# Second layer's paired projections: the next pair's weights prepared between the products of a pair, and the additions of h shared between GpSimd and VectorE

## The chip, the cores and the metric

The kernel runs on one core of a Trainium2 chip. The metric is the time of one execution on the device in microseconds (us); the median of three runs of the kernel before is 1481.52 us (1481.36 to 1482.64). The engines are TensorE (PE, with its weight loads as PEld), VectorE (DVE), ScalarE (ACT), GpSimd (POOL) and SyncE (SP), which here only issues DMAs. Each engine takes its instructions strictly in its own order; what one needs of another it waits for with a semaphore.

## The reference, cut to what matters

Two layers over 1024 latent and 256 context tokens of width 1024. Each layer normalises and modulates the tokens (h) and multiplies them by one wide input weight. Its columns feed four head groups (neighbourhood attention, latent attention, a spatial-gating MLP, a short convolution) and their gates:

```
hx = modulate(rms_norm(x, norm_g), sh_x, sc_x)
(a_q, a_k, a_v, a_g, b_cq, b_ckv, b_kr, b_g,
 c_u, c_v, c_g, d_b, d_c, d_h, d_g) = jnp.split(hx @ w_in, IN_SPLIT_POINTS, axis=-1)
...
out_d = short_conv(d_b, d_c, d_h, sc_w)
x_new = x + g_x * merge_branches((out_a, out_b, out_c, out_d), (a_g, b_g, c_g, d_g), w_out)
```

In the second layer only the latent rows are put out, so ten of these blocks of 256 columns (cg, dc, dh, db, dg, cq, ak, aq, bg, ag) are multiplied with the 1024 latent tokens alone. That stretch is what changes.

## The kernel before, in words

Features lie on the 128 partitions and tokens along the free axis. The latent tokens are two chunks of 512 (c = 0, 1), the context is chunk 2; h lies as tiles `H[c, kc]` for 8 feature blocks kc. Float32 products are made of three passes: every operand is split into a rounded part (hi, a cast on ACT) and the rest (lo, a subtraction on POOL or DVE; `split`, L362 and L367), and PE adds hi·hi, hi·lo and lo·hi in PSUM.

In the second layer a block of 256 columns and the two token chunks form a product of 2 by 2 blocks, which `proj2` computes with seven block products instead of eight (the scheme of Strassen and Winograd). A product is 12 matmuls of 128x512. For that the right sides have to be prepared once for all ten pairs, and the left sides (the weights) for each pair:

- Right: `right_parts(i)` (L702 on; the addition is L708) adds hi and lo of four tiles of h to full values, `right_sums(i)` (L711 on; L715) subtracts them into four new operands named "1" to "4", which are split again. i runs from 0 to 3. All these additions are on POOL, the subtractions on DVE.
- Left: the weights of a pair come as four quarters of 256 KB (L735, on SP's queue), DVE makes four sums of them (L739 to L742), and seven operands are split (`w_op`). Three pairs of buffers, named wh, wl and wr, hold them. The operands of products 0 to 3 are written ahead of the pair, those of 4 to 6 behind products 0, 2 and 3.

The seven products add into three PSUM banks (x_, y_, z_), with two copies by ACT and one by DVE between (L757), which the next product on the same bank has to wait for.

Ahead of the pairs stands a stretch that is written out by hand and whose matmuls are chained, so that PE keeps the order of the text: ckv for the three chunks, each with a normalisation (sums over squares on PE, L597; a power on POOL, L218, and three small operations on DVE, L220 to L223; a broadcast by transposes on PE, L176; a multiplication and a split, L601 to L604); `cv_gate` of c = 0 and 1 (L536 on DVE, L539 on POOL); ak for the context; ten tiles of av (`av_tile`, L569 and L571), with the preparation of the right sides among them. The rest is ordered by a scheduler that works from the order of the text and from dependencies. It fills each engine's queue when the program is built; on the chip nothing is reordered. Tiles of one tag share a fixed number of buffers (x 20, g 24, wr, wh, wl and st 2 each). PSUM has five banks of the kind b, so a matmul block waits for the evacuation of the fifth before it.

After the tenth pair (ag) the kernel goes on to the attention stage: the scaled-up weights, then keys and queries that were stored to DRAM and are read back by DMAs that POOL issues (L954, L962, L1006).

Of the kernel before, what the change touches and what calls it, by code (L numbers as in the profile page):

```python
# [11 lines left out]
F32R = mybir.dt.float32r  # L12
AF = mybir.ActivationFunctionType
ALU = mybir.AluOpType
# [35 lines left out]
V_NG, V_BM, V_QN, V_KV, V_LN, V_SC, V_FG = 0, 8, 32, 34, 35, 37, 43  # L50
# [46 lines left out]
def backbone(ctx: ExitStack, tc: tile.TileContext, a, yT, dbg=None):  # L97
# [85 lines left out]
    def f(ap):  # L183
        return ap.bitcast(F32)
# [241 lines left out]
    def layer(l, H):  # L426
# [262 lines left out]
                spill(scr["kr"][:, :, o:o + n].rearrange("h p n -> p h n"), f(st[64:128]))  # L689


        nop = [0]
        w_tags = ["wh", "wl", "wr"]

        def w_op(raw, lo_eng="pool"):
            t = T(w_tags[nop[0] % len(w_tags)], [2, 512], F32R)
            nop[0] += 1
            split(t[:, 0, :], t[:, 1, :], raw, lo_eng=lo_eng)
            return t.rearrange("p h (k n) -> p h k n", k=4)

        R = {}

        def right_parts(i):

            t = {}
            for k, (c, kc) in enumerate(((0, i), (1, i), (1, i + 4), (0, i + 4))):
                t[k] = T("x", [512])
                after(pool.tensor_tensor(t[k], f(H[c, kc][:, 0, :]), f(H[c, kc][:, 1, :]), ALU.add), last_split[0])  # L708
            R["11", i], R["21", i], R["22", i] = H[0, i], H[0, i + 4], H[1, i + 4]
            return t  # L710

# [13 lines left out]
                              skip_group_check=True)  # L725
                    n += 1

        def proj2(base, evac, mid={}, raw="x"):

            r = {}  # L730
            for j in range(2):
                t = T("st", [2, 512]) if raw == "st" else None
                for k in range(2):
                    r[j, k] = T("x", [512]) if t is None else t[:, k]
                    sp.dma_start(r[j, k], a["wtb"][l, BLOCKS.index(f"{base}{j}")][:, k * 512:(k + 1) * 512])  # L735
            qt = T("wr", [2, 512]) if "wr" not in w_tags else None
            q = [T("x", [512]) if qt is None else qt[:, k] for k in range(2)]
            a11, a12 = w_op(r[0, 0]), w_op(r[0, 1])
            dve.tensor_tensor(q[1], r[0, 0], r[1, 0], ALU.subtract)  # L739
            dve.tensor_tensor(r[1, 0], r[1, 0], r[1, 1], ALU.add)  # L740
            dve.tensor_tensor(q[0], r[1, 0], r[0, 0], ALU.subtract)
            dve.tensor_tensor(r[0, 1], r[0, 1], q[0], ALU.subtract)  # L742
            ops = {0: a11, 1: a12, 2: w_op(q[0], "dve"), 3: w_op(r[1, 0])}
            later = {0: (4, q[1], "dve"), 2: (5, r[0, 1], "dve"), 3: (6, r[1, 1], "pool")}
            x_, y_, z_ = PS("b", [512]), None, None

            def step(n, p, name, first=True):
                for fn in mid.get(n, []):
                    fn()
                product(p, ops[n], name, first)  # L750
                if n in later:
                    k, src, eng = later[n]
                    ops[k] = w_op(src, eng)

            def kept_copy(eng, p):
                t = T("tmp", [512])
                (eng.copy if eng is act else eng.tensor_copy)(t, p)  # L757
                return t

            step(0, x_, "11")  # L760
            m1 = kept_copy(act, x_)
            y_ = PS("b", [512])
            step(1, y_, "21")
            dve.tensor_tensor(m1, y_, m1, ALU.add)
            evac(0, m1, 0)
            step(2, x_, "2", False)
            u2 = kept_copy(act, x_)
            z_ = PS("b", [512])
            step(3, z_, "1")
            z5 = kept_copy(dve, z_)  # L770
            step(4, x_, "3", False)
            dve.tensor_tensor(z5, x_, z5, ALU.add)
            evac(1, z5, 1)
            step(5, z_, "22", False)
            dve.tensor_tensor(u2, z_, u2, ALU.add)
            evac(1, u2, 0)
            step(6, x_, "4", False)
            evac(0, x_, 1)

        def block_c(name, c, evac, **k):  # L780

# [5 lines left out]
        def standard():  # L787
# [51 lines left out]
            for j in range(2):  # L839
                proj(f"bg{j}", all_chunks, lambda c, p: act.activation(map_(2 + j, c), p, AF.Silu))  # L840

        def paired():
            wav = w_tok(a["wav"][l], 288, ("o", "o"), ("o", "o"))
            pe.chain(True)
# [18 lines left out]
                fns.pop(0)()  # L863
            av_tile(8, wav)
            late[-1].pop()()
            parts.append(right_parts(1))
            for t in (9, 4):
                av_tile(t, wav)
            cv_gate(1)
# [7 lines left out]
                av_tile(t, wav)  # L877
            pe.chain(False)
            av_windows()
            proj2("cg", lambda c, p, j: gate(c, p, 4 + j))  # L880
            park((4, 5))
            proj2("dc", lambda c, p, j: act.copy(map_(6 + j, c), p))
            kr = kr_rotate()
            z = {}

            def conv_in(c, p, j):
                z[j, c] = T("x", [512])
                dve.tensor_tensor(z[j, c], p, map_(6 + j, c), ALU.mult)

            proj2("dh", conv_in)  # L890
            kr_transpose(*kr)
            for j in range(2):
                w = [v[:, V_SC + 3 * j + i:V_SC + 3 * j + i + 1] for i in range(3)]
                for c in range(2):
                    m = map_(6 + j, c)
                    act.activation(m, z[j, c], AF.Copy, scale=w[1])
                    for d, s_, k in ((m[:, 1:], z[j, c][:, :511], 0), (m[:, :511], z[j, c][:, 1:], 2),
                                     (m[:, 0:1], z[j, 0][:, 511:], 0) if c else (m[:, 511:], z[j, 1][:, 0:1], 2)):
                        dve.scalar_tensor_tensor(d, s_, w[k], d, ALU.mult, ALU.add)

            def mulb(c, p, j):
                m = map_(6 + j, c)
                dve.tensor_tensor(m, p, m, ALU.mult)

            proj2("db", mulb)
            proj2("dg", lambda c, p, j: gate(c, p, 6 + j))
            park((6, 7))
            proj2("cq", cq_evac)
            proj2("ak", k_evac)
            proj2("aq", lambda c, p, j: q_evac(c, p, j, 0.125))  # L910
            cq_stats()
            w_tags.remove("wr")
            proj2("bg", lambda c, p, j: act.activation(map_(2 + j, c), p, AF.Silu))

        agw = []

# [8 lines left out]

        if last:
            ph = Phase("prj", ("o",))
            paired()
        else:
            standard()  # L930
            ag_weights()
# [535 lines left out]
        order = (0, 1) if last else (2, 0, 1)  # L1467
        if last:
            pe.chain(True)
            proj2("ag", lambda c, p, j: act.activation(map_(j, c), p, AF.Silu),  # L1470
                  {1: [mla_load], 6: [lambda: mla_keys(0)]})
# [218 lines left out]
```

## Time and profile before

| | us |
|---|---|
| runs: median (lowest, highest) | 1481.52 (1481.36, 1482.64) |
| profiled execution, its own time | 1482.33 |
| its span, first to last instruction | 1480.5 |
| PE busy in the span | 1398.0 (94%) |
| DVE busy | 867.8 (59%) |
| ACT busy | 607.6 (41%) |
| POOL busy | 500.0 (34%) |
| mean granted clock of TensorE | 0.988 |

The profile is of one execution. Times of rows are microseconds from the start of its span; 1.8 us of the execution lie outside the span. The stretch of this change goes from about 856 us (the first addition of h) to about 1143 us (the end of the tenth pair). A row of the timeline gives the start, the duration of the whole group, the engine, the line, the operation with its tiles, how many instructions are merged, and in brackets how long the engine was idle before it and who ended that. A granted clock of 1.00 is the upper of TensorE's two levels, 2.4 GHz, 0.50 is the lower, 1.2 GHz.

### The profile page before, as it was taken

What the parts mean: (1) busy time and instruction counts of PE and PEld (TensorE: products, weight loads), DVE (VectorE), ACT (ScalarE), POOL (GpSimd) and SP (SyncE); (2) the same over time, 40 slices, a digit from 0 to 9 for tenths busy, and PEclk for the clock granted to TensorE, in tenths of its full rate; (3) what the DMA queues carried; (4) which work ended last, traced back from release to release, by engine and by line L of the source; (5) the groups of instructions that cost most, each with busy time, mean ns of one, the idle gap of its engine ahead of it and who ended that gap; (6) DMA issues with size and microseconds to landing.
All of it is one profiled execution on the core that took longest, in us unless ns stands there. A gap on an engine that the chain in (4) does not pass through costs nothing.

```text
span 1480.5 us, 23128 instructions
## 1 busy us (share of the span) xinstructions
PE 1398.0 (94%) x8844; PEld 1174.1 (79%) x8844; DVE 867.8 (59%) x1923; ACT 607.6 (41%) x1371; POOL 500.0 (34%) x402
## 2 busy tenths in 40 slices
PE   4999999999998999999999998889998999999997
PEld 2788888988887877778888888667786777778887
DVE  5966648064017776674564746756644777665574
ACT  5611111121226665653443423433443666655533
POOL 2144334032220002436512365624525001065641
PEclk9999999999999999999999999899999999999999
DMA  9513324355442003756433112330439203286231
GB/s 355 187 44 131 110 92 162 107 179 173 157 107 37 1 23 74 181 149 168 136 114 121 35 60 92 110 101 32 164 128 255 30 8 73 84 181 162 88 137 63
DMA packets 86125, 170.64 MB, mean 115 GB/s; under 512 B 8704, under 2 KB 35328, under 8 KB 85888
## 3 DMA queue, kind: packets, MB, share of 16 engines
q1 hardware_dynamic: 68992, 140.86, 28.9%
q0 software_dynamic: 15936, 27.27, 9.3%
q8 instruction: 69, 1.13, 0.3%
q10 hardware_dynamic: 1088, 1.05, 0.2%
q14 instruction: 40, 0.33, 0.1%
HBM read 137.43 MB, written 35.91 MB: 117 GB/s over the span
## 4 chain that ended last, share of the span: by engine, by line
PE 78%; DVE 5%; POOL 4%; issue 4%; DMA 3%; ACT 3%; SPq 1%; DVEq 0%; POOLq 0%; ACTq 0%
PE psb L173 62%; PE psv L173 8%; PE pst L176 7%; PE pst L173 1%; POOL s L218 1%; POOL x L708 1%; DVE x L715 1%; POOL wl L367 1%; DMA x<-in_wtb 1%; DMA g<-scr_cq 1%; DVE s L1081 1%; DVE pt L970 1%; ACT g L1228 1%; DMA wr<-in_wtb 0%; POOL g L367 0%
## 5 line engine op out<-in xcount | busy, mean ns | idle before, releaser
L173 PE MATMUL psb<-g,wh 128*128 128x512 f32 (+1 forms) x2062 | 562.0, 367 | 16.1 <-ACT wh L362 11.1
L173 PEld LDWEIGHTS psb<-g,wh 128*128 128x128 f32 x2062 | 368.4, 189 | 88.8 <-ACT wh L362 12.6
L173 PE MATMUL psb<-g,wl 128*128 128x512 f32 (+1 forms) x1160 | 388.6, 368 | 2.5 <-ACT wl L362 1.2
L173 PEld LDWEIGHTS psb<-g,wl 128*128 128x128 f32 x1160 | 218.5, 189 | 42.8 <-ACT wl L362 1.8
L367 POOL TENSOR_TENSOR wl<-wr,wh 128x1024 fp32r<-128x1024 f32 (+2 forms) x45 | 108.0, 2403 | 196.9 <-ACT wh L362 195.6
L173 PE MATMUL psb<-g,st 128*128 128x512 f32 (+1 forms) x600 | 159.0, 382 | 9.3 <-ACT wl L1098 3.8
L1081 DVE TENSOR_REDUCE s<-psb 128x1 f32<-128x512 f32 (+1 forms) x200 | 117.4, 590 | 68.8 <-PE psb L173 66.7
L173 PE MATMUL psb<-g,g 128*128 128x256 f32 (+1 forms) x784 | 129.4, 305 | 2.5 <-ACT wh L1098 1.1
L173 PEld LDWEIGHTS psb<-g,st 128*128 128x128 f32 x600 | 95.6, 192 | 33.3 <-issue 6.5
L173 PE MATMUL psv<-pt,g 128*64 128x256 f32 (+1 forms) x1312 | 119.4, 331 | 0.6 <-ACT pt L972 0.5
L972 ACT COPY pt<-pst 128x512 f32<-128x512 f32 x116 | 67.9, 585 | 111.0 <-PE pst L176 110.2
L173 PEld LDWEIGHTS psb<-g,g 128*128 128x128 f32 x784 | 105.4, 191 | 9.5 <-issue 2.9
L340 DVE CUSTOM_DVE_ANT_0 tmp<-g,x 128x512 f32<-128x512 f32 x112 | 94.8, 896 | 22.1 <-POOL x L489 20.6
L173 PEld LDWEIGHTS psv<-pt,g 128*64 128x64 f32 x1312 | 79.3, 137 | 32.5 <-issue 8.6
L176 PE MATMUL pst<-ident,g 128*128 128x128 f32 x448 | 79.1, 278 | 11.3 <-ACT g L1228 6.3
L173 PE MATMUL psb<-g,wr 128*128 128x256 f32 (+1 forms) x418 | 79.8, 337 | 3.4 <-DMA g<-scr_cq 1.5
L970 DVE COPY pt<-pst 128x512 f32<-128x512 f32 x116 | 79.1, 683 | 6.7 <-PE pst L176 6.1
L364 POOL TENSOR_SCALAR wh<-wr 128x1024 fp32r<-128x1024 f32 x16 | 44.3, 2771 | 113.3 <-PE pst L176 75.3
L1414 DVE SCALAR_TENSOR_TENSOR x<-psb,modG,x 128x512 f32<-128x512 f32 (+1 forms) x48 | 29.5, 615 | 84.6 <-PE psb L173 43.6
L176 PEld LDWEIGHTS pst<-ident,g 128*128 128x128 f32 x448 | 54.0, 140 | 28.0 <-ACT g L1228 8.3
L362 ACT CAST wh<-wr 128x1024 fp32r<-128x1024 f32 (+2 forms) x39 | 38.2, 985 | 91.2 <-PE psb L173 68.8
L173 PEld LDWEIGHTS psb<-g,wr 128*128 128x128 f32 x418 | 63.8, 189 | 12.7 <-ACT wr L362 1.6
(252 smaller groups left out, 2185.8 us busy)
## 6 DMA issues: line engine op xcount, KB each, us to landing
g<-in_wmod SPq DMA_DIRECT2D x48, 512.0 KB, 4.7
wr<-in_wtb SPq DMA_DIRECT2D x28, 512.0 KB, 3.8
wr<-in_wout SPq DMA_DIRECT2D x27, 512.0 KB, 4.0
x<-in_wtb SPq DMA_DIRECT2D x40, 256.0 KB, 4.5
st<-in_nab SPq DMA_DIRECT2D x24, 384.0 KB, 3.4
x<-in_xT SPq DMA_DIRECT2D x32, 256.0 KB, 5.8
g<-scr_q POOLq DMA_DIRECT2D x32, 256.0 KB, 7.2
x<-x SPq DMA_DIRECT2D x24, 256.0 KB, 2.4
```

Of the source, the lines that this page charges most:

```text
L173: return self._next(nc.tensor.matmul(*p, **k))
L176: return self._next(nc.tensor.transpose(*p, **k))
L218: pool.tensor_tensor(r0, v, mhalf[:, :n], ALU.pow)
L340: dve.tensor_tensor_reduce(junk, w[:, hf * 512:hf * 512 + 512], crow[cond, hf], 1.0, 0.0, ALU.mult, ALU.add, part[:, i, cond, hf:hf + 1])
L362: act.copy(hi, raw)
L364: pool.tensor_scalar(hi, raw, 1.0, None, ALU.mult)
L367: m = (pool if lo_eng == "pool" else dve).tensor_tensor(lo, raw, f(hi), ALU.subtract)
L708: after(pool.tensor_tensor(t[k], f(H[c, kc][:, 0, :]), f(H[c, kc][:, 1, :]), ALU.add), last_split[0])
L970: dve.tensor_copy(dst, src)
L972: act.copy(dst, src)
L1081: dve.reduce_max(st["mx"][:, i:i + 1], s_, AX.X)
L1414: dve.scalar_tensor_tensor(xa, p, mod[l]["G"][:, fb, cond:cond + 1], xa, ALU.mult, ALU.add)
```

## The change

The change replaces `proj2` by a class `Pair` with steps `load`, `sums`, `op(n)`, `prep` and `run(nxt)`: while a pair runs, the next pair's weights are loaded behind product 1, its sums are made behind product 3 and its operands 0 to 3 are split behind products 4 to 6. The first pair (cg) is prepared as a whole in front of the right sides. The additions of h go to DVE and POOL in turn. The tenth pair (ag) is prepared during the ninth. The bodies of the convolution step move into functions without a change; the ninth pair uses the wr buffers too. In the text of the changed kernel `parts = [right_parts(0)]` still stands ahead of the ak block, and `parts = [right_parts(0), right_parts(1)]` follows behind the preparation of cg.

```
-                after(pool.tensor_tensor(t[k], f(H[c, kc][:, 0, :]), f(H[c, kc][:, 1, :]), ALU.add), last_split[0])
+                m = (pool if k % 2 else dve).tensor_tensor(t[k], f(H[c, kc][:, 0, :]), f(H[c, kc][:, 1, :]), ALU.add)
+                after(m, last_split[0] if k % 2 else gated.get(1, gated[0]))
...
-            a11, a12 = w_op(r[0, 0]), w_op(r[0, 1])
-            dve.tensor_tensor(q[1], r[0, 0], r[1, 0], ALU.subtract)
-            dve.tensor_tensor(r[1, 0], r[1, 0], r[1, 1], ALU.add)
-            dve.tensor_tensor(q[0], r[1, 0], r[0, 0], ALU.subtract)
-            dve.tensor_tensor(r[0, 1], r[0, 1], q[0], ALU.subtract)
...
+            def prep(self):
+                self.load()
+                self.sums()
+                for n in range(4):
+                    self.op(n)
+
+            def run(self, nxt=None):
+                evac = self.evac
+                todo = {0: [lambda: self.op(4)], 2: [lambda: self.op(5)], 3: [lambda: self.op(6)]}
+                if nxt:
+                    todo[1] = [nxt.load]
+                    todo[3].append(nxt.sums)
+                    todo[4] = [lambda: nxt.op(0)]
+                    todo[5] = [lambda: nxt.op(1)]
+                    todo[6] = [lambda: nxt.op(2), lambda: nxt.op(3)]
...
-            parts.append(right_parts(1))
+            pairs = {"cg": Pair("cg", lambda c, p, j: gate(c, p, 4 + j)),
...
+            pairs["cg"].prep()
+            parts = [right_parts(0), right_parts(1)]
...
+            for name, nxt in zip(names, names[1:]):
+                pairs[name].run(pairs[nxt])
+                for fn in behind_pair.get(name, []):
+                    fn()
+            return pairs["ag"]
```

POOL, from the last split of the av weights on (o are those, x the results of the additions of h, s the small tiles of the normalisations, wh and wl operands of cg). Before:

```order
L367 TENSOR_TENSOR o_8692<-wr_8697,o_8691 128x576
L708 TENSOR_TENSOR x_8869<-g_7640 128x512
L708 TENSOR_TENSOR x_8871<-g_8131 128x512
L708 TENSOR_TENSOR x_8873<-g_8151 128x512
L708 TENSOR_TENSOR x_8875<-g_7660 128x512
L708 TENSOR_TENSOR x_8981<-g_7645 128x512
L708 TENSOR_TENSOR x_8983<-g_8136 128x512
L708 TENSOR_TENSOR x_8985<-g_8156 128x512
L708 TENSOR_TENSOR x_8987<-g_7665 128x512
L218 TENSOR_TENSOR s_8665<-s_8663,mhalf_73 128x16
L218 TENSOR_TENSOR s_8819<-s_8759,mhalf_73 128x2
L218 TENSOR_TENSOR s_8912<-s_8793,mhalf_73 128x4
```

The same place in the changed kernel:

```order
L218 TENSOR_TENSOR s_8665<-s_8663,mhalf_73 128x16
L218 TENSOR_TENSOR s_8819<-s_8759,mhalf_73 128x2
L218 TENSOR_TENSOR s_8912<-s_8793,mhalf_73 128x4
L539 TENSOR_TENSOR x_8273<-x_8273,tmp_8854 128x512
L699 TENSOR_TENSOR x_8871<-g_8131 128x512
L699 TENSOR_TENSOR x_8875<-g_7660 128x512
L539 TENSOR_TENSOR x_8300<-x_8300,tmp_8866 128x512
L367 TENSOR_TENSOR wh_8994<-x_8981,wh_8994 128x512
L218 TENSOR_TENSOR s_8964<-s_8844,mhalf_73 128x4
L367 TENSOR_TENSOR wl_8997<-x_8983,wl_8997 128x512
L367 TENSOR_TENSOR wh_9003<-x_8985,wh_9003 128x512
L699 TENSOR_TENSOR x_9008<-g_8131 128x512
```

The powers of the normalisations (L218) have moved ahead of the additions; three additions (L699) and three splits of cg (L367) follow, and the last addition shown adds g_8131 a second time.

DVE, from the sums over squares of ckv's chunk 0 (s_8844) to the end of its power's refinement (s_8969), which PE's transposes of pst_8971 read; those stand at the same place of PE's order in both kernels, ahead of nine av tiles. Before:

```order
L597 TENSOR_SCALAR s_8844<-pst_8929 128x4
L604 TENSOR_TENSOR st_8925<-tmp_8791,st_8925 128x512
L220 SCALAR_TENSOR_TENSOR s_8966<-s_8844,s_8964 128x4
L221 TENSOR_TENSOR s_8966<-s_8966,s_8964 128x4
L223 SCALAR_TENSOR_TENSOR s_8969<-s_8966,s_8964 128x4
```

In the changed kernel the part up to the second weight sum comes first (L699 L699 L643 L601 L597 L737 L604 L738 L367), and then:

```order
L739 TENSOR_TENSOR x_8989<-x_8985,x_8981 128x512
L699 TENSOR_TENSOR x_9006<-g_7640 128x512
L220 SCALAR_TENSOR_TENSOR s_8966<-s_8844,s_8964 128x4
L699 TENSOR_TENSOR x_9010<-g_8151 128x512
L699 TENSOR_TENSOR x_9014<-g_7645 128x512
L699 TENSOR_TENSOR x_9018<-g_8156 128x512
L571 COPY tmp_8674<-psb_8935 128x32
L744 TENSOR_TENSOR x_8983<-x_8983,x_8989 128x512
L221 TENSOR_TENSOR s_8966<-s_8966,s_8964 128x4
L367 TENSOR_TENSOR wr_9000<-x_8989,wr_9000 128x512
L223 SCALAR_TENSOR_TENSOR s_8969<-s_8966,s_8964 128x4
```

The three small operations of the normalisation, which stood together, now have the sums and splits of cg and the additions of h around them.

SP, in the third pair (in_wtb are the weights, here of db; scr_kr is a store of the rotated key). Before:

```order
L559 DMA scr_kr_8230<-st_9807 64x2x512
L559 DMA scr_kr_8230<-st_9816 64x2x512
L559 DMA scr_kr_8230<-st_9823 64x2x256
L735 DMA x_9843<-in_wtb 128x512
L735 DMA x_9845<-in_wtb 128x512
L735 DMA x_9847<-in_wtb 128x512
L735 DMA x_9849<-in_wtb 128x512
```

In the changed kernel:

```order
L732 DMA x_9727<-in_wtb 128x512
L732 DMA x_9729<-in_wtb 128x512
L732 DMA x_9731<-in_wtb 128x512
L732 DMA x_9733<-in_wtb 128x512
L559 DMA scr_kr_8230<-st_9840 64x2x512
L559 DMA scr_kr_8230<-st_9849 64x2x512
L559 DMA scr_kr_8230<-st_9856 64x2x256
```

The loads of a pair have moved ahead of the stores that the pair before leaves behind.

## Rows read from the trace of the kernel before

**Rows 1.** Timeline of PE, 862 to 921 us.

```profile
874.34 0.69 PE L176 MATMUL pst<-ident,s 128*128 128x128 f32 x2 [3.38 <-DVE s L223]
...
880.06 0.69 PE L173 MATMUL psb<-g,wh 128*128 128x256 f32 x2
...
887.72 0.60 PE L176 MATMUL pst<-ident,s 128*128 128x128 f32 x4
888.08 6.64 PE L173 MATMUL psb<-o,g 128*128 128x288 f32 x48
894.65 1.97 PE L173 MATMUL psb<-tmp,g 128*64 128x128 f32 x32
896.54 22.65 PE L173 MATMUL psb<-o,g 128*128 128x288 f32 x168
```

**Rows 2.** Timeline of POOL, the same stretch.

```profile
859.86 8.52 POOL L708 TENSOR_TENSOR x<-g 128x512 f32<-128x512 f32 x6
868.34 2.91 POOL L218 TENSOR_TENSOR s<-s,mhalf 128x16 f32<-128x16 f32 x1
...
879.30 1.27 POOL L539 TENSOR_TENSOR x<-x,tmp 128x512 f32<-128x512 f32 x1 [1.39 <-DVE s L220]
```

**Rows 3.** Timeline of PE, 918 to 948 us.

```profile
930.29 5.24 PE L173 MATMUL psb<-g,wh 128*128 128x512 f32 x12 [5.02 <-ACT wh L362]
...
942.80 2.96 PE L173 MATMUL psb<-g,wl 128*128 128x512 f32 x12
```

**Rows 4.** By stretch, psb alone: us, busy PE, PEld, DVE, ACT, clock, DMA share, GB/s.

```profile
919.15:946.36 27.21, 17.59 (x61) 13.20 (x60) 1.06 (x3) 1.53 (x3) 0.75 0.50 165
946.36:1142.60 196.24, 186.52 (x789) 146.76 (x789) 32.34 (x49) 18.08 (x32) 1.00 0.42 126
```

**Rows 5.** Timeline of DVE, 875 to 962 us.

```profile
876.56 0.16 DVE L597 TENSOR_SCALAR s<-pst 128x4 f32<-128x4 f32 x1 [1.01 <-PE pst L173]
...
879.33 1.26 DVE L221 TENSOR_TENSOR s<-s,s 128x4 f32<-128x4 f32 x1
...
880.71 0.75 DVE L536 SCALAR_TENSOR_TENSOR tmp<-psb,vecs,v 128x512 f32<-128x512 f32 x1
...
895.79 1.62 DVE L536 SCALAR_TENSOR_TENSOR tmp<-psb,vecs,v 128x512 f32<-128x512 f32 x2 [0.40 <-PE psb L173]
...
924.86 1.37 DVE L739 TENSOR_TENSOR x<-x,x 128x512 f32<-128x512 f32 x1 [4.42 <-DMA x<-in_wtb]
...
937.58 0.68 DVE L367 TENSOR_TENSOR g<-x,g 128x512 fp32r<-128x512 f32 x1
```

**Rows 6.** Groups by line, 926 to 933 us: busy, mean ns of one.

```profile
L715 DVE TENSOR_TENSOR x<-x,x 128x512 f32<-128x512 f32 x2 | 3.5, 1764 | 0.0
L367 POOL TENSOR_TENSOR wh<-x,wh 128x512 fp32r<-128x512 f32 x2 | 3.4, 1724 | 0.0
...
L741 DVE TENSOR_TENSOR x<-x,x 128x512 f32<-128x512 f32 x1 | 0.7, 678 | 0.0
```

**Rows 7.** Who PE waited for, 940 to 1150 us: total, times, longest.

```profile
PE psb L173 <- ACT tmp L757: 2.6, 4, 0.7
PE psb L173 <- ACT wh L362: 2.0, 1, 2.0
PE psb L173 <- DMA g<-scr_cq: 1.5, 2, 1.1
...
PE psb L173 <- ACT wl L362: 1.2, 1, 1.2
PE psb L173 <- ACT wr L362: 1.2, 1, 1.2
PE psb L173 <- POOL wh L367: 0.9, 1, 0.9
```

**Rows 8.** Timeline of SP's issues from the first pair on.

```profile
946.75 13.15 SPq L465 DMA_DIRECT2D scr_m<-x  x4
```

**Rows 9.** Timeline of POOL in the tenth pair.

```profile
1126.25 2.29 POOL L954 DMA_DIRECT2D g<-scr_ck  x3
```

More of the change, by code (lines that the diff above doesn't have):

```diff
@@ L689, in kr_transpose @@
                 spill(scr["kr"][:, :, o:o + n].rearrange("h p n -> p h n"), f(st[64:128]))
[L692 to L699, printed above, removed]
         R = {}
@@ L726, in product @@
                     n += 1
[L728 to L737, printed above, removed]
-            a11, a12 = w_op(r[0, 0]), w_op(r[0, 1])
-            dve.tensor_tensor(q[1], r[0, 0], r[1, 0], ALU.subtract)
-            dve.tensor_tensor(r[1, 0], r[1, 0], r[1, 1], ALU.add)
-            dve.tensor_tensor(q[0], r[1, 0], r[0, 0], ALU.subtract)
-            dve.tensor_tensor(r[0, 1], r[0, 1], q[0], ALU.subtract)
[L743 to L778, printed above, removed]
@@ L840, in standard, with ag_pair, conv_in, conv @@
                 proj(f"bg{j}", all_chunks, lambda c, p: act.activation(map_(2 + j, c), p, AF.Silu))
+        def ag_pair():
+            return Pair("ag", lambda c, p, j: act.activation(map_(j, c), p, AF.Silu), {1: [lambda: mla_load()], 6: [lambda: mla_keys(0)]},
+                     ("wh", "wl"))
+        z = {}
+        def conv_in(c, p, j):
+            z[j, c] = T("x", [512])
+            dve.tensor_tensor(z[j, c], p, map_(6 + j, c), ALU.mult)
+        def conv():
+            for j in range(2):
+                w = [v[:, V_SC + 3 * j + i:V_SC + 3 * j + i + 1] for i in range(3)]
+                for c in range(2):
+                    m = map_(6 + j, c)
+                    act.activation(m, z[j, c], AF.Copy, scale=w[1])
+                    for d, s_, k in ((m[:, 1:], z[j, c][:, :511], 0), (m[:, :511], z[j, c][:, 1:], 2),
+                                     (m[:, 0:1], z[j, 0][:, 511:], 0) if c else (m[:, 511:], z[j, 1][:, 0:1], 2)):
+                        dve.scalar_tensor_tensor(d, s_, w[k], d, ALU.mult, ALU.add)
+        def mulb(c, p, j):
+            m = map_(6 + j, c)
+            dve.tensor_tensor(m, p, m, ALU.mult)
         def paired():
@@ L879, in paired @@
             av_windows()
[L880 to L913, printed above, removed]
+            names = list(pairs)
+            behind_pair = {"cg": [lambda: park((4, 5))], "dc": [lambda: kr.extend(kr_rotate())],
+                           "dh": [lambda: kr_transpose(*kr), conv], "dg": [lambda: park((6, 7))], "aq": [cq_stats]}
+            kr = []
+            for name, nxt in zip(names, names[1:]):
+                pairs[name].run(pairs[nxt])
+                for fn in behind_pair.get(name, []):
+                    fn()
+            return pairs["ag"]
         agw = []
@@ L927, in layer @@
             ph = Phase("prj", ("o",))
-            paired()
+            ag_run = paired()
         else:
@@ L1469, in layer @@
             pe.chain(True)
-            proj2("ag", lambda c, p, j: act.activation(map_(j, c), p, AF.Silu),
-                  {1: [mla_load], 6: [lambda: mla_keys(0)]})
+            ag_run.run()
             units[0].prep()
```

59 lines of the change are left out of this document (added).

## The prediction

> **What bounds the kernel now.** I looked first at how the time of PE goes by stretch, because PE is busy for 94% of the span: only where PE is idle, or runs at the lower clock, can a change of the order give time. In the stretch that changes there are four such places. The timeline of PE shows a wait of 3.38 us at 874.34 for the last operation of a normalisation on DVE (L223); what PE does between it and 880.06 goes at half speed [rows 1]. The timeline of POOL shows why: the power (L218) stands behind six additions of h that take 8.52 us [rows 2]. Then, from 919.15 to 946.36, there are only 61 matmuls of the first pair, 17.59 us busy at a mean granted clock of 0.75, with a wait of 5.02 us for a split of cg and twelve matmuls at 0.44 us where later twelve take 2.96 [rows 3, 4]. Behind 946.36 the clock is 1.00 and what is left is single waits, which the table of waits names [rows 7]. DVE, POOL and ACT bound nothing for long, but DVE and POOL set when the operands are ready. What follows behind the tenth pair has the same order in both kernels.
>
> The change is worked out against the profiled execution, 1482.33 us, which is 0.81 above the median of the runs; this is taken off at the end.
>
> **A: the first wait goes (+5.3 us; 4 to 5.5).** In the changed order the three powers stand ahead of all additions on POOL. Between 870.96 (874.34 less 3.38) and 880.06 PE spent 9.1 us [rows 1]. What is left: the square on ACT behind the last product, estimated at 0.6; two transposes and eight sums at full clock, estimated at 1.2 (874.34 to 880.06 is 5.7, less 3.9 for the gate's products at half speed leaves 1.8 at half speed, and some of it is latency); and the 32 small products of `cv_gate`, 1.97 us by the same 32 at full clock at 894.65 [rows 1]. That is 3.8, so 5.3 are saved, if the clock holds.
>
> **B: a second wait comes (-17.5 us; -7 to -21).** PE's next broadcast, the four transposes at 887.72 [rows 1], needs the L223 of chunk 0. In the kernel before nothing stood in its way. Now it does: the three small operations L220 to L223 are spread over DVE's work for cg and h (the piece of DVE's order above). DVE is through with the second evacuation of `cv_gate` (880.71 and 0.75 long) at 880.71 + 0.75 - 5.3 = 876.2 [rows 5], and PE comes to the transposes at 887.72 - 5.3 = 882.4. Between the two, up to and with L223, DVE's order has 13 operations of 128x512 with two inputs in SBUF (six additions of h, the four sums L737, L738, L739 and L744 of cg's weights, two splits, and L604), two that read PSUM (L643, L601) and five small ones. Alone the 13 take 0.68 each, the two at most as much, the small ones 0.16 [rows 5]. Beside them POOL has ten of its own kind: additions, gates, splits. And the two engines hold each other up: at 879.33 a 128x4 operation of DVE took 1.26 us while POOL worked on L539 from 879.30 to 880.57 [rows 2, 5], and in the one stretch where both worked at this without a pause, 926 to 933, DVE took 1.76 and POOL 1.72 for what DVE does in 0.68 alone [rows 6].
>
> So the small operations and the two from PSUM cost 5 x 0.16 + 2 x 0.68 = 2.2 us; of the 13, I price ten, as many as POOL has, at 1.72 and three at 0.68: 19.2. L223 ends at 876.2 + 21.4 = 897.6, and PE waits 15.2 us. The lower bound has none of them held up: 13 x 0.68 + 2.2 = 11.0, a wait of 4.8; the upper one all 13 at 1.76: 25.1, a wait of 18.9. After either PE comes back at the lower clock, which cost 5.24 - 2.96 = 2.3 us for the twelve matmuls at 930.29 [rows 3]; I add 2.3. I take the middle value, nearest to the rows at 926. In short, A cures a wait of three small operations behind additions on POOL, and B makes the same one on DVE, four times as long.
>
> The Trainium skill ("SBUF — State Buffer", section "Who interferes with whom") says that a DVE instruction with two SBUF inputs contends with a GpSimd one that reads SBUF, and that the one that comes second is blocked for the whole instruction of the other. It speaks against the change: additions shared between these two engines do not run side by side. The row at 879.33 agrees [rows 5]; by the rule as it stands the 13 and the ten would follow each other, 13 x 0.68 + 10 x 1.27 = 21.5 in place of 19.2, and the time would be 2.3 us longer than my forecast; the rows at 926 show a little less than that sum for a pair (1.72 to 1.76 against 1.95).
>
> That there are so many additions has one more reason: `right_parts(0)` stands twice in the changed text, so there are 20 additions in place of 16, ten on each engine, and four of the first ones are used by nobody.
>
> A and B together leave PE 12.2 us later: the last av tile, which ended at 919.2, ends at 931.4.
>
> **C: the first pair (+10.4 us; -5 to +12).** The 61 matmuls from 919.15 take 27.21 us; at 186.52 / 789 = 0.236 each [rows 4] they would take 14.4, so 12.8 are lost. The operands of cg are now prepared before the av tiles, and the two waits for splits of cg go. What can be late instead are the right sides: their chain on DVE went from the evacuations of the second gate, 895.79, to the last split, 938.26, in 42.5 us, of which DVE spent 4.42 waiting for weights [rows 5]. That wait goes; seven operations on cg leave the chain and about eight others (the additions, sums of the next pair) come in, which I count as even. It begins at 895.79 + 12.2 = 908.0 and ends at 908.0 + 42.5 - 4.4 = 946.1. PE needs the last right side for its 56th matmul, at 931.4 + 55 x 0.236 = 944.4. So it waits 1.7, and about 0.7 for a copy: 2.4 are lost in place of 12.8. The upper end has no wait for the right sides, the lower one is the third rival.
>
> **D: the other pairs (+7.0 us; 0 to 7.2).** Behind 946.36 PE waits 1.9 us for ACT's copies (2.6 less the first, 0.7), and 2.0, 1.2 and 1.2 for casts of weights and 0.9 for a split on POOL [rows 7]: 7.2. In the changed order the next pair's operands are cast while products 4 to 6 run, its product 0 comes between product 6 and what needs the copies, and its loads stand ahead of the stores that hold SP for 13.15 us after the first pair [rows 8]. I count 7.0.
>
> **E: the tenth pair (+1.0 us; 0 to 1.5).** The read-back DMAs issued by POOL (L954) come at 1126.25, behind the splits of ag [rows 9]; PE later waits 1.5 for a tile that comes back from scr_cq [rows 7]. ag's splits are now done a pair earlier, so the issues move ahead; I count two thirds.
>
> **Sum.** 5.3 - 17.5 + 10.4 + 7.0 + 1.0 = 6.2 us gained: 1482.33 - 6.2 - 0.81 = 1475.3, forecast 1475. Alone this case reaches from 1471 to 1479 (B's wait 4 us more or less).
>
> **Rivals.** First, DVE and POOL do not hold each other up here as they do at 926 (POOL often waits for casts by ACT, and leaves DVE alone). Then B's wait is 4.8 and 10.4 more are won: 1465. For it: in most of the stretch DVE's operations take 0.68, as at 937.58 [rows 5]. Against it: POOL's four additions in a row need nobody.
>
> Second, the change does not do what it says for the pairs: the casts are taken into ACT's order earlier, but the evacuations there (and the two buffers of each of the tags wh, wl and wr) keep them where they are, or one wait replaces another, as D's waits are all short. Then D is 0 and the time 1482: no change. For it: the waits are 0.6 to 2.0 long, each less than one cast and one split; against it: a whole pair's time lies between the preparation and the use.
>
> Third, slower: the right sides come late. From the second gate to their last split DVE has 31 operations of 128x512; the forecast has them at (946.1 - 908.0) / 31 = 1.23 us in the mean. At the 1.72 of 926 [rows 6] the last comes at 908.0 + 31 x 1.72 = 961.3, 16.9 after PE wants it in place of 1.7, so 15.2 are lost: C is -4.8 and the time 1490. It decides from a mean of 1.43 on, where the 6.2 are gone. For it: POOL has six splits and four additions of its own there; against it: in the kernel before the same chain, with much the same work on POOL, kept to about this 1.23.
>
> **How the numbers follow.** Forecast 0.52, first rival 0.20, second 0.20, third 0.08. Differences of less than 0.2%, 3 us, can hardly be told from none here. The forecast's own range lies on the faster side but for its upper end; with the first rival and a small part taken from its upper end, faster has 0.66; the second rival and that part make 0.24 for the same; the third and mishaps in the forecast's B make 0.10 for slower. The range goes from 1465, the first rival, to 1484, beyond the second; the third is left out.
>
> **What would show it.** A: no wait of PE at about 871 to 874 for L223. B: one single wait of about 15 us before the transposes at about 882, ended by L223 on DVE, a drop of the clock behind it, and 20 additions, with 128x512 operations of DVE above 1.2 us in the mean from 876 to 898. C: the first matmul of cg near 931 and hardly a wait before the fifth product. D: in the table of waits no casts of wh, wl and wr and at most a few copies. E: no wait for scr_cq. If the wait at 882 is under 8 us, B was wrong; if the waits of casts are still there, D was.

## The result, and the profile after

The changed kernel takes 1466.62 us in the median (1465.26 to 1471.75, four runs) against 1482.08 (1481.36 to 1486.38) for the kernel before; the ratio of the two is 0.9896, 95% interval 0.9865 to 0.9927, so between 10.8 and 20.0 us are won. The forecast was 1475 with a range of 1465 to 1484: the side was right and the time lies in the range, but the forecast gain of 7 us is less than half of the 15.5 that came.

The profiled execution has a span of 1463.5 us, 17.0 less than before. Not all of that is the change. PE's sums over squares of ckv stand at the same place of its order in both kernels, far ahead of the first moved instruction. Before, and then after (start, duration, engine, line, operation):

```profile
808.58 0.95 PE L173 MATMUL pst<-ones,tmp 128*128 128x2 f32 x8
```

```profile
806.00 0.95 PE L173 MATMUL pst<-ones,tmp 128*128 128x2 f32 x8
```

The profiled execution after is 2.6 us ahead there; over all kernels of this study this row stands between 806.00 and 810.86. So stretches are compared below from this row on, one execution of each kernel: it is 671.9 us to the end before and 657.5 after, 14.4 won. The timeline of PE after, to hold against [rows 1, 3]:

```profile
868.23 0.38 PE L176 MATMUL pst<-ident,s 128*128 128x128 f32 x2
...
869.32 1.97 PE L173 MATMUL psb<-tmp,g 128*64 128x128 f32 x32
871.22 0.50 PE L173 MATMUL psb<-g,wh 128*128 128x256 f32 x2
...
875.41 3.43 PE L173 MATMUL psb<-o,g 128*128 128x288 f32 x24
891.95 1.09 PE L176 MATMUL pst<-ident,s 128*128 128x128 f32 x4 [13.10 <-DVE s L223]
892.68 8.93 PE L173 MATMUL psb<-o,g 128*128 128x288 f32 x48
901.54 1.97 PE L173 MATMUL psb<-tmp,g 128*64 128x128 f32 x32
903.44 22.66 PE L173 MATMUL psb<-o,g 128*128 128x288 f32 x168
925.93 2.94 PE L173 MATMUL psb<-g,wh 128*128 128x512 f32 x12
...
938.53 0.50 PE L173 MATMUL psb<-g,wr 128*128 128x512 f32 x1 [1.24 <-ACT g L362]
...
942.79 1.66 PE L173 MATMUL psb<-g,wl 128*128 128x512 f32 x6 [0.79 <-ACT tmp L776]
```

The wait at 874.34 has gone and the gate's 32 products take 1.97 us. The wait that was forecast for the four transposes is there, 13.10 us, ended by L223 on DVE, and the 48 products behind it take 8.93 us where they took 6.64, at a mean granted clock of 0.71. Then cg's products run from 925.93 with two short waits, where before there were holes.

What DVE did while PE waited, the timeline of DVE after, and of POOL beside it:

```profile
877.57 0.67 DVE L601 TENSOR_TENSOR tmp<-tmp,pst 128x512 f32<-128x512 f32 x1
...
880.18 1.75 DVE L367 TENSOR_TENSOR wl<-x,wl 128x512 fp32r<-128x512 f32 x1
881.86 1.75 DVE L739 TENSOR_TENSOR x<-x,x 128x512 f32<-128x512 f32 x1
883.53 1.75 DVE L699 TENSOR_TENSOR x<-g 128x512 f32<-128x512 f32 x1
885.20 1.22 DVE L220 SCALAR_TENSOR_TENSOR s<-s,s 128x4 f32<-128x4 f32 x1
886.34 4.01 DVE L699 TENSOR_TENSOR x<-g 128x512 f32<-128x512 f32 x3
...
891.65 0.15 DVE L223 SCALAR_TENSOR_TENSOR s<-s,s 128x4 f32<-128x4 f32 x1
```

```profile
876.72 1.75 POOL L367 TENSOR_TENSOR wh<-x,wh 128x512 fp32r<-128x512 f32 x1
878.43 1.47 POOL L218 TENSOR_TENSOR s<-s,mhalf 128x4 f32<-128x4 f32 x1
...
883.02 6.79 POOL L699 TENSOR_TENSOR x<-g 128x512 f32<-128x512 f32 x4
```

The additions that were to be shared stand side by side from 883 to 890: 1.70 us each on POOL, up to 1.75 on DVE, and even L220 on 128x4 elements takes 1.22 in place of 0.16. L601, which has one input in PSUM, keeps its 0.67 beside POOL's split at 876.72.

The busy time by stretch, matmuls into psb alone (columns as in [rows 4]):

```profile
925.93:942.79 16.86, 14.79 (x62) 10.95 (x60) 1.38 (x3) 1.55 (x3) 1.00 0.78 256
942.79:1129.45 186.66, 184.35 (x790) 147.54 (x790) 31.51 (x48) 17.72 (x32) 1.00 0.45 137
```

The waits of PE from 940 to 1150 after, which answer to [rows 7] (total, times, longest):

```profile
PE psb L173 <- ACT tmp L776: 1.6, 3, 0.8
PE psb L173 <- ACT st L1089: 1.5, 1, 1.5
PE psb L173 <- DVE s L1117: 0.8, 1, 0.8
PE psb L173 <- ACT wl L1124: 0.7, 1, 0.7
PE psb L173 <- DVE g L996: 0.3, 1, 0.3
```

The casts of wh, wl and wr (L362), the splits of wh and wl (L367) and scr_cq are no longer in the table; the rows from L1089 on belong to the work behind the tenth pair, which comes earlier now. What came behind the tenth pair is seen in the first products with st, before and after:

```profile
1147.52 3.57 PE L173 MATMUL psb<-g,st 128*128 128x512 f32 x9 [1.48 <-ACT st L1063]
...
1164.07 2.42 PE L173 MATMUL psb<-g,st 128*128 128x256 f32 x9 [0.73 <-ACT wl L1098]
```

```profile
1132.52 2.28 PE L173 MATMUL psb<-g,st 128*128 128x512 f32 x9 [1.48 <-ACT st L1089]
...
1147.22 2.42 PE L173 MATMUL psb<-g,st 128*128 128x256 f32 x9 [0.72 <-ACT wl L1124]
```

The same nine products of 128x512 behind the same wait: before, after two more waits for scr_cq, they run at the lower clock (granted 0.55 from 1146.4 to 1154, and 1.00 at the same place after).

| term | forecast | measured | read from |
|---|---|---|---|
| A, first wait | +5.3 | +6.3 | PE is at the four transposes at 891.95 - 13.10 = 878.85, 8.9 before 887.72, less the 2.6 |
| B, second wait and clock | -17.5 | -15.8 | 13.1, and 11.5 in place of 8.8 us from the transposes to the av tiles behind the gate |
| C, first pair | +10.4 | +10.3 | 16.9 in place of 27.2 us |
| D, other pairs | +7.0 | +9.5 | 186.7 in place of 196.2 us |
| E, tenth pair and what follows | +1.0 | +3.7 | from the end of the pair to the nine products with st of 128x256 (1147.22 after, 1164.07 before): 17.8 in place of 21.5 us |
| sum | +6.2 | +14.0 | 14.4 from the row at 806.00 |

### The profile page after: what moved, and what is told of

Read it like the earlier page. It is cut to its first block, busy times and chain, and to the rows that moved or that the text cites. A ratio compares the mean times of both kernels' runs of the same rounds, so it can differ in the third digit from the quotient of the medians.

```text
span 1463.5 us, 23118 instructions
## 1 busy us (share of the span) xinstructions
PE 1388.0 (95%) x8844; PEld 1168.6 (80%) x8844; DVE 873.9 (60%) x1933; ACT 607.5 (42%) x1371; POOL 492.7 (34%) x396
## 5 line engine op out<-in xcount | busy, mean ns | idle before, releaser
L173 PE MATMUL psb<-g,wh 128*128 128x512 f32 (+1 forms) x2044 | 553.7, 365 | 4.1 <-ACT x L501 1.4
L173 PEld LDWEIGHTS psb<-g,wh 128*128 128x128 f32 x2044 | 363.3, 188 | 72.8 <-ACT g L420 2.6
L367 POOL TENSOR_TENSOR wl<-wr,wh 128x1024 fp32r<-128x1024 f32 (+2 forms) x45 | 107.9, 2400 | 196.6 <-ACT wh L362 195.4
L173 PE MATMUL psb<-g,wr 128*128 128x256 f32 (+1 forms) x448 | 86.0, 338 | 1.2 <-ACT g L362 1.2
L364 POOL TENSOR_SCALAR wh<-wr 128x1024 fp32r<-128x1024 f32 x16 | 44.4, 2773 | 113.4 <-PE pst L176 52.2
L173 PEld LDWEIGHTS psb<-g,wr 128*128 128x128 f32 x448 | 69.8, 189 | 10.8 <-ACT g L362 1.7
L362 ACT CAST wh<-wr 128x1024 fp32r<-128x1024 f32 (+2 forms) x37 | 37.0, 1005 | 88.2 <-PE psb L173 66.1
```

The lines of the kernel that those rows point to most:

```text
L173: return self._next(nc.tensor.matmul(*p, **k))
L362: act.copy(hi, raw)
L364: pool.tensor_scalar(hi, raw, 1.0, None, ALU.mult)
L367: m = (pool if lo_eng == "pool" else dve).tensor_tensor(lo, raw, f(hi), ALU.subtract)
```

## The experiments

The ratio behind a time is that to the kernel before, timed together with it, with its 95% interval. The four runs of the changed kernel spread over 6.5 us, so a difference of 3 to 6 us from its median is uncertain by itself; the time from the row of the sums to the end (657.5 us in the changed kernel, one execution of each) is given beside it. Several of these kernels have two or three more lines ahead of the code in question: L225 is L223 there, L364 and L369 are L362 and L367.

The first question was what the 13.10 us are, and whether they can be had back. Four kernels (before: 1482.64).

**One right_parts(0) (e1_one_sum).** 1463.39 us (ratio 0.9865, 0.9844 to 0.9885).

```
-            parts = [right_parts(0)]
             block_c("ak1", 2, lambda c, p: k_evac(c, p, 1), lo_eng="dve")
```

> Left out against the changed kernel: the first of the two right_parts(0), whose four sums nobody uses (two additions on VectorE, two on GpSimd); nothing else in the text. The built order moves more than that: cg's loads and three of its sums come ahead of the second chunk's gate, and between that gate and L223 seven 128x512 operations with two SBUF inputs stand on VectorE, not 13. Theory 1 (the wait at the transposes is the length of VectorE's queue in front of L223): the wait falls from 13.1 to about 6 us; the right sides' chain on VectorE starts earlier but is not shorter, so half of that comes back as a wait in the first pair, and the time falls by 3 to 6 us, to 1460 to 1463. Theory 2 (VectorE's work as a whole bounds this stretch, wherever it stands): the wait at the transposes turns into a wait at the fifth product, and only the two additions count: 1464 to 1466. Theory 3 (the wait is GpSimd's power being late): the wait stays at 12 to 13.

The wait is 8.71 us, still ended by L223: less than 13.1, but more than the 6 of theory 1. The time is 3.2 lower in the median and 5.9 from the common row, as theory 1 had it. Here L220 waited 0.81 for GpSimd's power at the end of it: with the queue on VectorE shorter, the one on GpSimd comes near.

**The chain kept together (e2_chain_whole).** 1462.70 us (0.9859, 0.9839 to 0.9879).

```
             late[-1].pop()()
+            hold[0] = last_r[0]
...
-                dve.tensor_tensor(q[1], r[0, 0], r[1, 0], ALU.subtract)
-                dve.tensor_tensor(r[1, 0], r[1, 0], r[1, 1], ALU.add)
+                after(dve.tensor_tensor(q[1], r[0, 0], r[1, 0], ALU.subtract), hold[0])
+                after(dve.tensor_tensor(r[1, 0], r[1, 0], r[1, 1], ALU.add), hold[0])
...
-                after(m, last_split[0] if k % 2 else gated.get(1, gated[0]))
+                after(m, last_split[0] if k % 2 else gated.get(1, hold[0] or gated[0]))
```

> Against the changed kernel: cg's sums and the second right_parts(0) and (1) on VectorE are ordered behind the last power refinement (L223 of chunk 0); all work is kept, the double sums too. Between the gate and L223 stand three 128x512 operations with two SBUF inputs, not 13. Theory 1: the wait at the transposes falls from 13.1 to 3 to 5 us and the clock stays up; since ten operations now come after it on VectorE (about 14 us), the right sides are ready only some 4 us earlier, and the time falls by about 4 us to 1462. Theory 2 (VectorE's work as a whole bounds): the wait reappears in full at the first pair and the time stays at 1465 to 1467. Theory 3 (GpSimd's power is late): the wait at the transposes stays over 10.

`last_r[0]` is the last operation of the last refinement, L223 of chunk 0. All the work is kept, only its order on VectorE differs. PE's waits (timeline of PE):

```profile
884.52 0.62 PE L176 MATMUL pst<-ident,s 128*128 128x128 f32 x4 [2.50 <-DVE s L225]
...
927.73 0.50 PE L173 MATMUL psb<-g,wh 128*128 128x512 f32 x1 [1.22 <-ACT g L364]
930.53 0.73 PE L173 MATMUL psb<-g,wl 128*128 128x512 f32 x2 [2.30 <-ACT wl L364]
932.96 0.79 PE L173 MATMUL psb<-g,wr 128*128 128x512 f32 x1 [1.19 <-ACT g L364]
```

2.50 us in place of 13.10, and the clock stays up there (1.00 from 884.5 to 891); the order was the cause. But only 3.9 us of it reach the end (5.1 from the common row), as expected: the ten operations come later, and the first pair waits again, 4.7 us in the three waits shown. Behind the last of them the clock falls: ten matmuls at 933.55 take 4.47 us, where ten take 2.59 at the same place of the changed kernel (938.96).

**Both (e3_both).** 1459.32 us (0.9842, 0.9822 to 0.9862): the edits of the two kernels above together.

> Both edits together: one right_parts(0) only, and cg's sums and the additions on VectorE ordered behind L223 of chunk 0. One 128x512 operation with two SBUF inputs (L604) is left between the gate and L223. Theory 1: wait at the transposes 0 to 3 us, the right sides' chain ends 5 to 7 us earlier than in the changed kernel, time 1458 to 1461. Theory 2: PE waits 10 us or more in the first pair instead, time 1463 to 1465.

No wait is left at the transposes; 4.9 us are left in the first pair, and the same ten matmuls take 4.47 us there too. Theory 2, that VectorE's work is the bound wherever it stands, is refuted (it wanted a wait of 10 us or more, and 1463 to 1465); but of the 15.8 us of B only 7.3 came out (9.4 from the common row); the rest stands in the first pair.

**All additions on GpSimd (e4_adds_pool).** 1472.17 us (0.9932, 0.9915 to 0.9949), 5.6 slower than the changed kernel.

```
-                m = (pool if k % 2 else dve).tensor_tensor(...)
+                after(pool.tensor_tensor(...), last_split[0])
```

> The changed kernel with all 20 additions on GpSimd (the halving undone, the double right_parts(0) kept). Four additions stand ahead of the 128x16 power and eight ahead of chunk 0's power on GpSimd. Theory 1: the queue in front of the refinement only changes engines; the wait at the transposes is 10 to 14 us, ended by L223 all the same, and the time 1462 to 1468. Rival (halving the additions is what won the time in the first pair): the right sides come later, the fifth product waits 10 us or more and the time is 1474 or above.

The wait is 11.89 us, and this time DVE itself waits for POOL (timeline of DVE):

```profile
892.10 0.16 DVE L220 SCALAR_TENSOR_TENSOR s<-s,s 128x4 f32<-128x4 f32 x1 [10.56 <-POOL s L218]
```

So the queue only changed engines, as theory 1 said of the wait; its time was missed by 4 us. From the common row it is 4.0 slower than the changed kernel. The first pair takes 21.3 us in place of 16.9, with 4.3 in two waits for right sides, a part of what the rival said; and 1.3 us are lost at the nine products of 128x256 with st (3.69 in place of 2.42), although PE's waits behind the tenth pair are those of the changed kernel.

The second question was what the rest of the change is worth. Three kernels take it apart.

**Nothing but cg prepared ahead (e6_not_ahead).** 1481.09 us (0.9991, 0.9982 to 1.0001; before 1482.58).

```
-                pairs[name].run(pairs[nxt])
+                pairs[name].run()
                 for fn in behind_pair.get(name, []):
                     fn()
+                pairs[nxt].prep()
```

> The changed kernel, but only cg is prepared ahead: every later pair is loaded, summed and split behind the pair before it, as in the kernel before. Theory 1 (the single waits of the later pairs go because their operands are prepared between the products, and with them the restarts of the PE): the waits for casts of wh, wl and wr return behind the first pair, 7 to 9.5 us, and the read-back in the tenth pair costs 1 to 2 again: 1475 to 1478, with the wait of about 13 before the transposes unchanged. Rival (those waits went because the whole stretch lies differently, or because cg was prepared ahead): 1465 to 1469.

The largest miss of the study: 14.5 us slower than the changed kernel in the median, not 8 to 11. The waits came back as [rows 7] had them (timeline of PE, three of them), and the read-back on POOL stands behind ag's splits again:

```profile
974.26 0.73 PE L173 MATMUL psb<-g,wr 128*128 128x512 f32 x2 [1.19 <-ACT wr L362]
...
997.64 1.07 PE L173 MATMUL psb<-g,wh 128*128 128x512 f32 x2 [2.05 <-ACT wh L362]
...
1142.95 1.19 PE L173 MATMUL psb<-g,wl 128*128 128x512 f32 x4 [0.83 <-POOL wl L367]
```

```profile
1126.00 1.76 POOL L367 TENSOR_TENSOR wh<-x,wh 128x512 fp32r<-128x512 f32 x1
1127.70 2.29 POOL L981 DMA_DIRECT2D g<-scr_ck  x3
```

From the row of the sums to the end it takes 670.7 us, 13.2 more than the changed kernel. That is as much as D and E together in the table above (9.5 + 3.7), but it lies otherwise: 12.1 from the end of the first pair to the end of the tenth, 2.0 behind it, and 0.9 less ahead. And A, B and C together, which this kernel keeps (its wait at the transposes is 13.10 too), are worth 1.3 us here by the ratio (-0.1 to 2.7), where the table gives 0.8.

**Only ag late (e11_ag_late).** 1474.10 us (0.9946, 0.9933 to 0.9960; before 1482.70), 7.5 slower than the changed kernel and 1 above the range expected.

```
+                pairs[name].run(pairs[nxt] if nxt != "ag" else None)
                 ...
+                if nxt == "ag":
+                    pairs[nxt].prep()
```

> The changed kernel with the tenth pair (ag) alone loaded and split behind the ninth, as before; the other pairs are prepared ahead. Theory (the read-back DMAs on GpSimd stand behind ag's splits, and their lateness costs the waits for scr_cq and afterwards the lower clock): about 3.7 us for that and 2 for the two waits inside the tenth pair, 1471 to 1473. Rival (the read-back is late for another reason, or hidden): 1467 to 1469.

A wait for scr_cq is back with 0.54 us and, at the place of the other, one of 0.39 for the rest of a key on DVE (L1047); the nine products with st take 3.56 us again, and inside the tenth pair there are 1.19 and 0.79. From the row of the sums to the end it takes 663.3 us, 5.8 more than the changed kernel, 5.4 of them up to the nine products of 128x256 with st: nearly half of what preparing ahead is worth lies in the last pair. The rival is refuted.

**The power first (e8_power_first).** 1480.42 us (0.9985, 0.9976 to 0.9994): the kernel before with A alone.

```
-                after(pool.tensor_tensor(...), last_split[0])
+                after(pool.tensor_tensor(...), last_pow[0] if i < 2 else last_split[0])
```

> The kernel before, with one edit: the additions of the first two right_parts on GpSimd are ordered behind the last power ahead of them; pairs, weights and everything else as before. Theory (term A of the forecast alone): the wait of 3.4 us for L223 at the two transposes goes, PE comes to the four transposes about 6 us earlier at the upper clock, and since the right sides' chain starts from the second gate it all moves along: 1475 to 1478. Rival (the first pair waits for weights and splits of cg whose time does not depend on it): the gain comes back as a longer wait in the first pair, 1480 to 1482.

PE is ready for the four transposes 6.3 us earlier, so A is right; then it waits 2.13 us there (the three operations of the normalisation, L222 to L225 there, took 1.25, 1.19 and 1.18 us beside GpSimd's additions), and the casts of cg, which wait for their weights, hold it up for 3.79 and 5.23 us as before. 2.2 us are left (0.9 to 3.6): the rival's mechanism, and its time.

The third question was whether sharing work between VectorE and GpSimd gives anything. Two kernels on top of "Both", and one that tests the order of the chain.

**All 16 additions on VectorE (e7_both_dve).** 1456.20 us (0.9822, 0.9809 to 0.9835), 3.1 faster than with half of them on GpSimd (3.7 from the common row).

```
-                m = (pool if k % 2 else dve).tensor_tensor(...)
-                after(m, last_split[0] if k % 2 else gated.get(1, hold[0]))
+                m = dve.tensor_tensor(...)
+                after(m, gated.get(1, hold[0]))
```

> The kernel of e3_both with all 16 additions on VectorE instead of half of them on GpSimd. Theory A (side by side the two engines hold each other up for nearly the whole of an instruction, so sharing gives hardly anything): VectorE takes 0.68 us per addition when GpSimd is quiet, eight more are 5.4 us, and about as much is saved on the operations that were held up; the time is within 2 us of e3_both, 1457 to 1461. Rival (they run side by side and the sharing halves the time): the right sides come 5 us or more later, 1464 or above.

**The rests of the right operands on VectorE as well (e10_all_dve).** 1449.54 us (0.9786, 0.9771 to 0.9800), the fastest kernel here: 33 us under the kernel before (1482.70) and 17 under the changed one. It is 2.5 us below the range expected of it; the kernel above was 0.8 below its own.

```
-                split(r[:, 0, :], r[:, 1, :], t[o], lo_eng="dve" if name in "12" else "pool")
+                split(r[:, 0, :], r[:, 1, :], t[o], lo_eng="dve")
```

> The kernel of e7_both_dve with the rests (lo) of all 16 new right operands on VectorE too; in e7_both_dve eight of them are on GpSimd, and beside them VectorE's operations take 1.7 to 1.8 us instead of 0.68. Theory A (side by side the two give nothing): eight more operations on VectorE at 0.68 are 5.4 us, about as much is saved on those held up, and the 3.5 us that PE waits for the last rest on VectorE shrinks; 1452 to 1456. Rival (GpSimd's share is real work taken off VectorE): the right sides come 4 us later and the time is 1459 or above.

The timeline of DVE in the first of these (GpSimd works on rests of right operands at that time), and then in the second, shows the same kind of work:

```profile
912.17 1.69 DVE L369 TENSOR_TENSOR g<-x,g 128x512 fp32r<-128x512 f32 x1
913.78 1.79 DVE L709 TENSOR_TENSOR x<-x,x 128x512 f32<-128x512 f32 x1
915.49 1.78 DVE L369 TENSOR_TENSOR g<-x,g 128x512 fp32r<-128x512 f32 x1
```

```profile
911.40 2.48 DVE L369 TENSOR_TENSOR g<-x,g 128x512 fp32r<-128x512 f32 x4
913.81 0.68 DVE L709 TENSOR_TENSOR x<-x,x 128x512 f32<-128x512 f32 x1
914.41 0.68 DVE L369 TENSOR_TENSOR g<-x,g 128x512 fp32r<-128x512 f32 x1
915.01 0.68 DVE L709 TENSOR_TENSOR x<-x,x 128x512 f32<-128x512 f32 x1
```

From the second gate to VectorE's last rest the chain takes 37.2 us in "Both" (894.46 to 931.69), 34.9 with the additions (892.54 to 927.42) and 31.3 with the rests as well (892.17 to 923.48): VectorE got more to do twice and was done sooner each time, and the rival is refuted in both. But the two steps gain in different ways. In "Both" VectorE stands idle for 3.5 of the 37.2 us, nearly all of it in one wait for additions on GpSimd:

```profile
921.87 1.76 DVE L709 TENSOR_TENSOR x<-x,x 128x512 f32<-128x512 f32 x1 [3.13 <-POOL x L701]
```

Without it the chain is 33.7 us, so what the first step took away is this wait, and VectorE was busy a little longer. In the other two kernels the chain has no idle time; there it is the operations themselves that became shorter, by more than the eight new ones cost. The busy time of the whole stretch in the last kernel (us, then PE, PEld, DVE, ACT and POOL busy, clock, DMA share, GB/s):

```profile
856.00:936.00 80.00, 80.00 (x538) 73.06 (x538) 62.10 (x111) 30.06 (x57) 27.73 (x20) 1.00 0.31 106
```

PE is busy for all of the 80 us at full clock, so no wait is left to take out there.

**Right sides first (e9_rights_first).** 1460.92 us (0.9847, 0.9834 to 0.9860): no better than "Both".

```
+                on_dve = i == 3 or k % 2 == 0
...
-                after(dve.tensor_tensor(t[o], t[p_], t[q_], ALU.subtract), gated[1])
+                hold[0] = after(dve.tensor_tensor(t[o], t[p_], t[q_], ALU.subtract), gated[1])
```

> The kernel of e3_both with two edits to the right sides' chain on VectorE: the additions of the last right_parts are all on VectorE (in e3_both VectorE waited 3.1 us for the two on GpSimd), and dc's three weight sums are ordered behind the last subtraction of the right sides. If that chain is what the first pair still waits for (4.9 us in e3_both, in three waits), the time is 1454 to 1457 and PE waits 0 to 2 us there. Rival (the casts on ScalarE, which take their turn behind those of the right sides, or dc's operands, now later, hold PE up instead): 1458 to 1461.

VectorE's chain took 29.4 us (895.24 to 924.67) in place of 37.2, but the longest of PE's three waits in the first pair (1.44, 1.59 and 3.71) is now for a rest of cg's own weights on GpSimd (timeline of PE, then of POOL): it stands behind four rests of right sides that came late together.

```profile
932.93 5.46 PE L173 MATMUL psb<-g,wl 128*128 128x512 f32 x16 [3.71 <-POOL wl L369]
```

```profile
922.97 7.01 POOL L369 TENSOR_TENSOR o<-x,o 128x512 fp32r<-128x512 f32 x4 [8.78 <-ACT o L364]
...
931.17 1.70 POOL L369 TENSOR_TENSOR wl<-x,wl 128x512 fp32r<-128x512 f32 x1
```

That is the rival, on GpSimd rather than on ScalarE: the wait leaves VectorE's queue and comes up in GpSimd's. Another 1 us is lost behind the tenth pair, at the nine products with st (3.32 us in place of 2.28).

## Why the prediction was right or wrong

**A** held: no wait, the gate at full clock. It was 1.0 too small, and outside its 4 to 5.5, mostly because the square on ACT, for which 0.6 us were set aside, is not on PE's path: the transposes follow the last product at once (868.23), and 3.0 us later PE is at the ak products (871.22), where 3.8 were counted. (The group of six additions in [rows 2] is a part of eight, which began at 856.31; no term hangs on it.)

**B** held in place, cause and nearly in size: 13.1 us in place of 15.2, and 2.7 for the clock in place of 2.3. VectorE's 13 operations took 15.7 us and not 19.2, 1.20 in the mean: about half of them were held up, not ten. GpSimd did not pause between 871.30 and 889.81, but three of the 13 ran beside its power at 878.43 and took 0.68 to 0.78, its split at 876.72 fell beside VectorE's readings of PSUM, and the last two ran when its additions had ended. The 2.1 us by which the wait came out shorter are a sum of two misses: L223 came 17.3 us after the gate's second evacuation and not 21.4, but PE reached the transposes 4.3 us after it and not 6.2. That the order is the cause is shown by "The chain kept together"; that the second right_parts(0) is a part of it, by "One right_parts(0)".

**C** held to 0.1 us, with a wait of 1.24 for a right side and 0.79 for the copy where 1.7 and 0.7 stood. VectorE's chain from the second gate to its last split took 38.0 us (902.69 to 940.66), and 38.1 were counted; but its make-up was not the one counted, so that the two agree so closely is partly luck. The wait for weights was to go whole, and one for dc's weights was left (timeline of DVE after):

```profile
933.58 0.69 DVE L737 TENSOR_TENSOR x<-x,x 128x512 f32<-128x512 f32 x1 [1.71 <-DMA x<-in_wtb]
```

**D and E** are the steps that failed: their terms were too small by 2.5 and 2.7 us, two thirds of the 7.8 us by which the forecast's sum falls short of the measured one. Both were priced by the length of waits alone: 7.0 "of 7.2", and two thirds of 1.5. As a count of waits D held: 7.9 us in eight waits before (one of 0.63 for a split of wl on POOL is not in the forecast's list), 0.8 in two after, behind 942.79. But the same products then also take 2.2 us less of busy time (186.52 us for x789 [rows 4] against 184.35 for x790). About 0.1 us of it stands behind each wait: two matmuls take 0.73 us behind the wait of 1.19 for wr, and 0.63 elsewhere. The rest was not taken apart; that it goes with the waits is inferred from the two profiles.

In E the two waits went whole, 1.5 us, and the products with st took 1.9 us less at the upper clock, which the forecast had at nothing. A price of a wait has to take in what PE does just after it; B's did, D's and E's did not, and for both their upper bounds were no bounds. But that the waits for scr_cq brought the clock down is not shown. The same nine products in "Nothing but cg prepared ahead", behind two such waits (0.32 and 0.60 us), and then in "Right sides first", which has none:

```profile
1149.79 2.27 PE L173 MATMUL psb<-g,st 128*128 128x512 f32 x9 [1.43 <-ACT st L1090]
```

```profile
1126.43 3.32 PE L173 MATMUL psb<-g,st 128*128 128x512 f32 x9 [1.48 <-ACT st L1092]
```

In the first the clock fell only later, at the nine products of 128x256 (3.69 us in place of 2.42). So what brings the clock down behind the tenth pair stays open, and with it 1.9 of E's 3.7 us.

**The first rival** gave 1465, close to the time that came, but its mechanism is refuted: VectorE and GpSimd do hold each other up, and the wait was 13.1, not 4.8. The forecast's own case reached from 1471 to 1479. That 1466.62 lies in the range is luck: the range was drawn down to 1465 for this rival. **The second** (D is 0) is refuted by "Nothing but cg prepared ahead". **The third** did not occur: the chain of the right sides had a mean near the forecast one.

So the two halves of the change did not share the gain. Preparing the pairs ahead is worth 13 to 15 us (13.2 from the common row, 14.5 by the medians); moving additions to VectorE and cg to the front gains and loses nearly the same. That the loss was B's is shown by "The chain kept together" and "Both"; that as much can be had back, by the last kernel with the rests on VectorE too.

## What to carry to other kernels

When work is moved forward on an in-order engine, look for short chains that another engine waits for, and keep them together: three operations of 0.16 us behind a dozen others cost PE 13 us. Price a wait with what PE loses behind it, and a whole stage by the time between two rows that both kernels share, not by the span. Before sharing work between VectorE and GpSimd, compare in the trace what a pair takes side by side with what VectorE takes for both: here 1.70 to 1.79 us against 2 x 0.68 = 1.36.

## What the hardware showed that was not expected

Moving work from GpSimd to VectorE made VectorE faster through its chain (34.9 us with the additions, 31.3 with the rests of the right operands as well), since an operation with two inputs in SBUF takes 0.68 us alone and 1.7 to 1.8 beside GpSimd's. What is added does not depend on the size: in the changed kernel L739 on 128x512 takes 1.75 in place of 0.68 and L220 on 128x4 takes 1.22 in place of 0.16, 1.07 and 1.06 more, while one instruction of GpSimd takes 1.27 alone. So small operations suffer most. This agrees in kind with the Trainium skill, "SBUF — State Buffer", section "Who interferes with whom", by which the one that comes second waits for the whole instruction of the other; the measured delay is a little less than that. The section leaves out operations with only one input in SBUF, and L601 at 877.57 agrees: it keeps its 0.67 us beside a split on GpSimd.
